# Where weights start, and how many rows the norm factors have, in a two-block fp32 transformer kernel

## The chip, the cores and the metric

The kernel runs on one core of one Trainium2 chip. The metric is the device time of one execution in microseconds. Each timed run gives one such time; the profiled execution is one more run, recorded by the hardware profiler, and it has its own time.

## The reference

Two blocks work on a sequence of 256 tokens of width 1024, in fp32.

```python
def first_block(x, ...):          # one stream
    h = h + hybrid_mixer(rmsnorm(h), w_in, ...)     # dilated attention + state space scan, gated
    h = h + swiglu(rmsnorm(h), w_ffn_in, w_ffn_out) # hidden width 2816
    return rmsnorm(h, final_norm_w)

def second_block(x, c, ctx, c_ctx, ...):            # two streams, x and ctx, and two layers
    for l in range(2):
        mx, mc = split(silu(c) @ w_mod[l] + b_mod[l]), split(silu(c_ctx) @ w_mod[l] + b_mod[l])
        x  = x  + 0.5 * mx[2] * swiglu_2(modulate(rms_norm(x),  mx[0], mx[1]), *ffn1)
        xc = xc + 0.5 * mc[2] * swiglu_2(modulate(rms_norm(xc), mc[0], mc[1]), *ffn1)
        # even layer: windowed attention with sinks, and differential attention:
        #   softmax(q1 k1) - lam * softmax(q2 k2), times v, then rms_norm(y_b, b_sub_norm)
        # odd layer: latent attention (ranks 768 and 256), and neighbourhood attention with a bias table
        # queries and keys of every head are normed: t * rsqrt(mean(t*t) + 1e-6) * gain, then rotated
        ...                                          # out projection, then a second swiglu_2 per stream
```

## The kernel before, in words

**Products.** Activations lie transposed, with features on the 128 partitions and tokens along the row. Every linear layer is computed in three passes of TensorE: a weight and an activation are each split into a rounded part and the rest, and `mm3_k` (L139 to L141) multiplies high by high, high weight by the activation's rest, and the weight's rest by high. In these matmuls the weight block of 128 by 128 is the stationary operand, which is loaded, and the activations are the moving operand, of 256 columns for one stream and 512 for both. In the value units (`v_units`, L1165 to L1167) it is the other way: the weights move, 256 or 320 columns of them, and the activations are loaded.

**Weights.** A weight slab of 128 by 1024 comes by a DMA of the SP queue into one of five buffers (`wraw`, L113). `split_w` casts the high part on ScalarE (L120) and subtracts on VectorE (L121) into one of five pairs of buffers, `wh` and `wl`.

**Units.** A unit is one slab with the outputs that it makes. `run` issues units in order and prepares the slabs of the next two or three. With two streams, the first units (`head`) and the last ones (`edge`) are issued one stream at a time, so that a stream can start while the other isn't ready; all units between take both streams in one matmul of 512 columns.

**Where tiles lie.** A tile's place in SBUF follows from the order in which pools and tiles are declared. `both_acts` declares two tiles that hold both streams side by side (`comb`), from 450 us on; a single stream is half of them. Once the context is no longer needed, `alone` cuts one-stream tiles from the same memory, 48 numbers (192 bytes) further in. The first block's mixer uses tiles of its own. A small `gap` tile after the weights shifts all that is declared behind it.

**Head norms.** `HeadNorm` squares a head's outputs, sums them by matmuls of two columns (L1047), turns the sums to factors, transposes these (L1056), and `finish` spreads each factor over its head's 64, 96 or 128 rows by a matmul (L1071): a selector of zeros and ones (`sel`, 48 rows) is the stationary operand, the factors (`rh`, 48 rows: high parts from row 0, rests from row 32) move, 256 columns. VectorE multiplies. These matmuls are issued among those of the next units.

**Attention.** Steps of heads are woven into one another. `softmax_tail` writes exponentials into one of eight tiles `e`. In the differential attention four heads' outputs are normed by `normed`, which has a square root on ScalarE; ScalarE loads another function table between exponentials and roots (ACT_TABLE_LOAD). In the neighbourhood attention `load_bias` brings a head's table by four DMAs on the SP queue (L1614) and adds a mask on GpSimd (L1615); the scores take it on VectorE (L1623). A scheduler sets the final order on each engine from dependences and buffers.

Of the kernel before, what the change touches and what calls it, by code (L numbers as in the profile page):

```python
# [8 lines left out]
F32 = mybir.dt.float32  # L9
F32R = mybir.dt.float32r  # L10
# [6 lines left out]
T = 256  # L17
# [31 lines left out]
class Unit:  # L49


    def __init__(self, src, at, n, body, streams=None, lin=None, wide=False):
        self.src, self.at, self.n, self.body, self.streams, self.lin = src, at, n, body, streams, lin
        self.wide = wide
# [14 lines left out]
class Builder:  # L69
    def __init__(self, ctx, tc, A):  # L70
        self.tc, self.nc, self.A, self.ctx = tc, tc.nc, A, ctx
        nc = self.nc
        self.cst = self.pool(ctx, "cst", 1)
        self.raw_p = self.pool(ctx, "raw", 5)
        self.w_p = self.pool(ctx, "wsplit", 5)

        self.gap(self.pool(ctx, "gap", 1), 320)
        self.tp = self.pool(ctx, "tmp", 10)
        self.small = self.pool(ctx, "small", 2)
        self.comb, self.one_p, self.single = None, None, False  # L80
        self.ps = ctx.enter_context(tc.tile_pool(name="ps", bufs=4, space=PSUM))
        self.pa = ctx.enter_context(tc.tile_pool(name="pa", bufs=2, space=PSUM))
        self.pt = ctx.enter_context(tc.tile_pool(name="pt", bufs=2, space=PSUM))
        self.dram = ctx.enter_context(tc.tile_pool(name="scratch", bufs=1, space=DRAM))
        self.X, self.ACT, self.acc, self.bg, self.deferred = {}, {}, {}, [], []

        self.ones = self.cst.tile([128, 128], F32, name="ones")
        nc.vector.memset(self.ones, 1.0)
        self.cols = self.cst.tile([128, NCOL], F32, name="cols")
        self.ident = self.cst.tile([128, 128], F32, name="ident")  # L90
# [22 lines left out]
        self.nc.sync.dma_start(t[:, :src.shape[1]], src)  # L113
        return t

    def split_w(self, raw, f):
        nc = self.nc
        h = self.w_p.tile([128, 1024], F32R, name="wh")
        lo = self.w_p.tile([128, 1024], F32R, name="wl")
        nc.scalar.copy(h[:, :f], raw[:, :f])  # L120
        nc.vector.tensor_tensor(lo[:, :f], raw[:, :f], h[:, :f].bitcast(F32), op=ALU.subtract)  # L121
        return h, lo
# [79 lines left out]
    def run(self, items, streams, done=None, ko=0, ahead=2):  # L202
# [5 lines left out]
        ready = {}  # L208

        def prepare(i):  # L210
            if i >= len(units) or i in ready:
                return
            u = units[i]
            f = u.src.shape[2]
            ready[i] = [self.split_w(self.load_raw(u.src[j]), f) for j in range(u.at, u.at + u.n)]

        last = {}
        for i, u in enumerate(units):
# [46 lines left out]
        two = len(streams) > 1  # L265
        n, tail, i = len(units), [], 0
        head = ko or (3 if two else 1)
        edge = 0
        while edge < n and sum(u.n for u in units[n - edge - 1:]) <= 3:
            edge += 1  # L270
        for item in items:
# [3 lines left out]
            j, m = i, 0  # L275
            if not two and i < head:

                j = i + 1 if i + 1 < head else n
                prepare(i)
            while j < n and (j < (head if i < head else i + 1) or m + units[j].n <= ahead + 1):  # L280
                prepare(j)
                m += units[j].n
                j += 1
# [804 lines left out]
def head_selectors(K, pool, width, rows, n):  # L1088

    nc, A = K.nc, K.A  # L1090
    at, n2 = COLS[f"sum{width}"]
    sums = K.cols[:rows, at:at + n2]
    raw = K.raw_p.tile([128, 1024], F32, name="wraw")
    sel = pool.tile([48, n * 128], F32R, name=f"sel{width}")
    nc.scalar.dma_start(raw[:48, :n * 128], A[f"sel{width}"])
    nc.vector.tensor_copy(sel, raw[:48, :n * 128])
    return sums, sel


def stacked(K, pool):  # L1100

    zero = K.t1("zero")
    K.nc.vector.memset(zero, 0.0)
    ring = []
    for i in range(4):
        ring.append(pool.tile([48, T], F32R, name=f"rh{i}"))
        K.nc.scalar.copy(ring[i], zero[:48])
    return ring


# [70 lines left out]
def mix_ab(K, streams):  # L1181
    nc, A = K.nc, K.A
    ctx = ExitStack()
# [10 lines left out]
    at = {"x": 0, "c": 256}  # L1194
# [4 lines left out]
    ring = stacked(K, rp)  # L1199
# [42 lines left out]
    sp = K.pool(sx, "abs", 1)  # L1242
# [131 lines left out]
    def normed(po):  # L1374
        yb = sp.tile([128, 4, 128], F32, name="yb", bufs=2)
        nc.scalar.copy(yb, po.rearrange("p (h e) -> p h e", h=4))
        sq = sp.tile([128, 4, 128], F32, name="ybs", bufs=1)
        ss = sp.tile([128, 4], F32, name="yss", bufs=2)


        nc.vector.tensor_scalar(sq, yb, 2.0 ** 64, -2.0 ** 64, op0=ALU.min, op1=ALU.max)
        nc.vector.scalar_tensor_tensor(sq, sq, 2.0 ** -64, sq, op0=ALU.mult, op1=ALU.mult)
        nc.vector.tensor_reduce(out=ss, in_=sq, axis=AX.X, op=ALU.add)
        fin = sp.tile([128, 4], F32, name="fin", bufs=2)
        nc.vector.tensor_scalar(fin, ss, 2.0 ** 64, 2.0 ** -32, op0=ALU.is_lt, op1=ALU.mult)
        nc.vector.tensor_scalar(ss, ss, 1.0 / 128.0, 1e-6 * 2.0 ** -64, op0=ALU.mult, op1=ALU.add)
        nc.vector.reciprocal(ss, ss)
        nc.scalar.activation(ss, ss, AF.Sqrt)
        nc.vector.tensor_tensor(ss, ss, fin, op=ALU.mult)
        nc.vector.tensor_tensor(yb, yb, ss.unsqueeze(2).to_broadcast([128, 4, 128]), op=ALU.mult)  # L1390
        return yb
# [19 lines left out]
def mix_cd(K, streams):  # L1411
    nc, A = K.nc, K.A
    ctx = ExitStack()
# [24 lines left out]
    at = {"x": 0, "c": 256}  # L1438
# [5 lines left out]
    ring = stacked(K, tp)  # L1444
# [3 lines left out]
    raw = {("q", "x"): v8[:, 0:6], ("k", "x"): d8[:, 0:2], ("k", "c"): d8[:, 2:4]}  # L1448
# [105 lines left out]
    sp = K.pool(sx, "cds", 1)  # L1554
# [50 lines left out]
    biases = {}  # L1605

    def load_bias(hd):
        bias = biases[hd] = sp.tile([128, 2, T], F32, name="bias", bufs=4)
        for t in range(2):
            for rr in range(2):  # L1610
                r = 2 * t + rr
                src = bass.AP(tensor=rpb.tensor, offset=rpb.offset + (hd * 7 + 3 - r) * 127 + 63,
                              ap=[[56 * 127 - 1, 64], [127, 4], [1, 64]])
                nc.sync.dma_start(bias[64 * rr:64 * rr + 64, t].rearrange("p (r c) -> p r c", r=4), src)  # L1614
        nc.gpsimd.tensor_tensor(bias, bias, dmask.unsqueeze(1).to_broadcast([128, 2, T]), op=ALU.add)  # L1615
# [140 lines left out]
def constants():  # L1756
    import numpy as np
    f = np.float32
    c = {}
    i = np.arange(128)  # L1760
# [13 lines left out]
    for g, (c0, n, off, d) in enumerate(((0, 383, 255, 1), (384, 255, 127, 4), (640, 255, 127, 16))):  # L1774
        u = np.arange(n)
        oh[np.where((off - u >= 0) & (off - u <= 128), bucket(np.clip(off - u, 0, 128) * d), 32), c0 + u] = 1.0
    c["onehot"] = oh
    sel = np.zeros((8, 512), f)
# [1 line left out]
        sel[h, h * 64:h * 64 + 64] = 1.0  # L1780
    c["sel"] = sel
    for name, rows, n in (("sel64", [64, 64], 5), ("sel96", [64, 32], 4)):
        sel = np.zeros((48, n, 128), f)
        for b in range(n):
            at = 0
            for e, r in enumerate(rows[:2]):
                sel[[2 * b + e, 32 + 2 * b + e], b, at:at + r] = 1.0
                at += r
        c[name] = sel.reshape(48, n * 128)
    t = np.arange(T)  # L1790

    def rope(dim):
# [129 lines left out]
```

## Time and profile before

| | us |
|---|---|
| timed runs | 2482.21, 2473.56, 2483.57 |
| their median | 2482.21 |
| profiled execution | 2473.19 |
| its span, first to last instruction | 2471.4 |

The page gives busy time by engine and the chain of waits that ended last. The mean granted TensorE clock is 0.985 of full speed. In the timeline each row is one instruction (or a group of equal ones), with start and duration; matmuls are pipelined, so the time of one is read from its start to the next one's start. PE is TensorE's matmuls, PEld its weight loads. In names such as `48*128 48x256` the first pair is the rows and columns of the stationary tile, the second the moving operand.

### The profile page before, as it was taken

How to read it: one execution, taken by the hardware profiler on the slowest of the kernel's cores; microseconds unless marked ns; L12 is line 12 of the kernel's file. 1: busy time of each engine (PE TensorE's matmuls, PEld its weight loads, DVE VectorE, ACT ScalarE, POOL GpSimd, SP SyncE). 2: the span in 40 equal slices, each digit the busy share in tenths (PEclk: the TensorE clock that was granted, in tenths of full speed). 3: DMA queues.
4: the chain of work that ended last, by engine and by line, in shares of the span. 5: the costliest groups of instructions: out<-in, count | busy, mean ns of one | idle time of the engine just before them, and what ended most of it. 6: DMA issues, size and time to landing. Idle time of an engine off the chain costs nothing.

```text
span 2471.4 us, 38395 instructions
## 1 busy us (share of the span) xinstructions
PE 2415.3 (98%) x15104; PEld 2101.6 (85%) x15104; DVE 1642.8 (66%) x3016; ACT 1064.7 (43%) x1934; POOL 34.3 (1%) x56
## 2 busy tenths in 40 slices
PE   7999999999999999999999999999999999999999
PEld 6998999999988888886498888888888888876999
DVE  5767787787865666778757666656555555667655
ACT  4566565535632222535743222243222234555443
POOL 3000000000000000000000000000000000000000
PEclk9999899999999999999899999999999999999999
DMA  9455455676454554341014555534555422233554
GB/s 271 153 154 157 134 175 174 212 251 225 148 177 136 170 173 144 112 139 52 1 52 154 165 159 162 165 108 142 180 166 171 150 87 84 100 97 86 169 195 133
DMA packets 113157, 363.38 MB, mean 147 GB/s; under 512 B 21186, under 2 KB 23562, under 8 KB 112976
## 3 DMA queue, kind: packets, MB, share of 16 engines
q1 hardware_dynamic: 109232, 352.58, 45.1%
q0 software_dynamic: 2176, 5.09, 0.9%
q10 hardware_dynamic: 1568, 3.25, 0.4%
q8 instruction: 119, 1.95, 0.3%
q14 instruction: 62, 0.51, 0.1%
HBM read 359.33 MB, written 3.36 MB: 147 GB/s over the span
## 4 chain that ended last, share of the span: by engine, by line
PE 70%; DVE 3%; ACT 2%; issue 1%; DMA 0%; ACTq 0%; DVEq 0%
PE pm L139 20%; PE pm L140 20%; PE pm L141 20%; PE pt L1140 1%; PE pa L1047 1%; PE pm L1339 1%; PE pt L1071 1%; PE pa L1592 1%; DVE wl L121 1%; PE pm L1600 1%; PE pa L1355 1%; PE pm L1279 1%; PE pa L1316 0%; PE pm L1622 0%; PE pm L1165 0%
## 5 line engine op out<-in xcount | busy, mean ns | idle before, releaser
L139 PE MATMUL pm<-ah,wh 128*128 128x256 f32 (+2 forms) x3096 | 1002.9, 326 | 13.1 <-ACT ah L370 10.7
L140 PE MATMUL pm<-al,wh 128*128 128x256 f32 (+2 forms) x3096 | 997.4, 323 | 1.1 <-DVE al L371 1.0
L141 PE MATMUL pm<-ah,wl 128*128 128x256 f32 (+2 forms) x3096 | 996.1, 322 | 0.0
L120 ACT CAST wh<-wraw 128x1024 fp32r<-128x1024 f32 (+4 forms) x535 | 541.0, 1014 | 946.0 <-PE pm L140 750.3
L121 DVE TENSOR_TENSOR wl<-wraw,wh 128x1024 fp32r<-128x1024 f32 (+4 forms) x535 | 627.5, 1176 | 228.3 <-ACT wh L120 225.8
L139 PEld LDWEIGHTS pm<-ah,wh 128*128 128x128 f32 (+1 forms) x3096 | 590.1, 192 | 67.8 <-ACT ah L370 12.3
L140 PEld LDWEIGHTS pm<-al,wh 128*128 128x128 f32 (+1 forms) x3096 | 591.9, 191 | 49.0 <-issue 2.7
L141 PEld LDWEIGHTS pm<-ah,wl 128*128 128x128 f32 (+1 forms) x3096 | 592.2, 191 | 46.6 <-issue 2.3
L140 PE MATMUL pm<-hl,wh 128*128 128x512 f32 (+1 forms) x934 | 312.6, 335 | 0.0
L139 PE MATMUL pm<-hh,wh 128*128 128x512 f32 (+1 forms) x934 | 312.1, 334 | 0.0
L141 PE MATMUL pm<-hh,wl 128*128 128x512 f32 (+1 forms) x934 | 312.1, 334 | 0.0
L1001 DVE SCALAR_TENSOR_TENSOR junk<-wraw,cactc 128x1024 f32<-128x1024 f32 x112 | 137.2, 1225 | 183.1 <-DMA wraw<-w_mod 183.0
L1001 DVE SCALAR_TENSOR_TENSOR junk<-wraw,cactx 128x1024 f32<-128x1024 f32 x144 | 176.1, 1223 | 48.8 <-DMA wraw<-w_mod 46.2
L139 PEld LDWEIGHTS pm<-hh,wh 128*128 128x128 f32 x934 | 175.7, 188 | 18.7
L140 PEld LDWEIGHTS pm<-hl,wh 128*128 128x128 f32 x934 | 175.7, 188 | 18.6
L141 PEld LDWEIGHTS pm<-hh,wl 128*128 128x128 f32 x934 | 175.8, 188 | 18.4
L125 ACT CAST hh<-g 128x512 fp32r<-128x512 f32 (+1 forms) x113 | 59.1, 525 | 228.4 <-DVE g L428 228.4
L428 DVE TENSOR_TENSOR g<-g,pm 128x512 f32<-128x512 f32 (+1 forms) x113 | 64.0, 567 | 55.6 <-PE pm L141 54.1
L126 DVE TENSOR_TENSOR hl<-g,hh 128x512 fp32r<-128x512 f32 (+1 forms) x113 | 63.9, 567 | 0.3
L458 DVE SCALAR_TENSOR_TENSOR xc<-pm,mcol0c,xc 128x256 f32<-128x256 f32 x56 | 26.9, 481 | 53.5 <-PE pm L141 53.3
L424 ACT ACTIVATE g<-pm 128x512 f32<-128x512 f32 (+1 forms) x116 | 55.9, 486 | 2.0 <-PE pm L141 2.0
L1140 PEld LDWEIGHTS pt<-ident,e 128*128 128x128 f32 x272 | 30.7, 145 | 22.0 <-issue 18.6
(425 smaller groups left out, 2260.0 us busy)
## 6 DMA issues: line engine op xcount, KB each, us to landing
wraw<-w_mod SPq DMA_DIRECT2D x144, 512.0 KB, 4.0
wraw<-f1g SPq DMA_DIRECT2D x44, 512.0 KB, 3.9
wraw<-f1u SPq DMA_DIRECT2D x44, 512.0 KB, 4.2
wraw<-f2g SPq DMA_DIRECT2D x44, 512.0 KB, 3.6
wraw<-f2u SPq DMA_DIRECT2D x44, 512.0 KB, 3.6
wraw<-f1d SPq DMA_DIRECT2D x32, 512.0 KB, 3.9
wraw<-f2d SPq DMA_DIRECT2D x32, 512.0 KB, 3.6
wraw<-w_xbc SPq DMA_DIRECT2D x24, 512.0 KB, 3.7
```

Of the source, the lines that this page charges most:

```text
L120: nc.scalar.copy(h[:, :f], raw[:, :f])
L121: nc.vector.tensor_tensor(lo[:, :f], raw[:, :f], h[:, :f].bitcast(F32), op=ALU.subtract)
L125: self.nc.scalar.copy(h, src)
L126: self.nc.vector.tensor_tensor(lo, src, h.bitcast(F32), op=ALU.subtract)
L139: nc.tensor.matmul(out, h[:, c], ah, start=first, stop=False)
L140: nc.tensor.matmul(out, h[:, c], al, start=False, stop=False)
L141: nc.tensor.matmul(out, lo[:, c], ah, start=False, stop=last)
L424: nc.scalar.activation(half(g["g"], s), p, AF.Silu)
L428: nc.vector.tensor_tensor(t, t, p, op=ALU.mult)
L458: self.nc.vector.scalar_tensor_tensor(x, p, gate, x, op0=ALU.mult, op1=ALU.add)
L1001: nc.vector.scalar_tensor_tensor(junk, raw, 1.0, K.cact[s], op0=ALU.mult, op1=ALU.mult, accum_out=K.mcol[layer, s][:, j:j + 1])
L1140: nc.tensor.transpose(p[:, j * 128:(j + 1) * 128], b, K.ident)
```

## The change

The buffers of split weights grow from 1024 to 1088 numbers per row. A unit that takes one stream from the tiles of both (with two streams: units of one stream, and the head and edge units; with one stream: units whose activations are half of `comb`) gets its weights 16 numbers, 64 bytes, further into the buffer. The gap tile shrinks from 320 to 64 bytes. The selectors and factors of the head norms become tiles of 128 rows, zero beyond the rows used before; the selector's host table grows with them. The square in `normed` takes a tile of the ring `e` in place of its own buffer, and the bias tables have three buffers in place of four.

```diff
-        self.gap(self.pool(ctx, "gap", 1), 320)
+        self.gap(self.pool(ctx, "gap", 1), 64)
...
-    def split_w(self, raw, f):
+    def split_w(self, raw, f, at=0):
         nc = self.nc
-        h = self.w_p.tile([128, 1024], F32R, name="wh")
-        lo = self.w_p.tile([128, 1024], F32R, name="wl")
+        h, lo = (self.w_p.tile([128, 1088], F32R, name="w" + n)[:, at:at + 1024] for n in "hl")
...
-            ready[i] = [self.split_w(self.load_raw(u.src[j]), f) for j in range(u.at, u.at + u.n)]
+
+            if two:
+                alone = len(u.streams or streams) == 1 or i < head or i >= n - edge
+            else:
+                alone = self.comb and not self.single and u.lin and u.lin[0] == self.acts
+            ready[i] = [self.split_w(self.load_raw(u.src[j]), f, 16 if alone else 0) for j in range(u.at, u.at + u.n)]
...
-    sel = pool.tile([48, n * 128], F32R, name=f"sel{width}")
-    nc.scalar.dma_start(raw[:48, :n * 128], A[f"sel{width}"])
-    nc.vector.tensor_copy(sel, raw[:48, :n * 128])
+    sel = pool.tile([128, n * 128], F32R, name=f"sel{width}")
+    nc.scalar.dma_start(raw[:, :n * 128], A[f"sel{width}"])
+    nc.vector.tensor_copy(sel, raw[:, :n * 128])
...
-        ring.append(pool.tile([48, T], F32R, name=f"rh{i}"))
-        K.nc.scalar.copy(ring[i], zero[:48])
+        ring.append(pool.tile([128, T], F32R, name=f"rh{i}"))
+        K.nc.scalar.copy(ring[i], zero)
...
-        sq = sp.tile([128, 4, 128], F32, name="ybs", bufs=1)
+        sq = sp.tile([128, 512], F32, name="e", tag="e", bufs=8).rearrange("p (h e) -> p h e", h=4)
...
-        bias = biases[hd] = sp.tile([128, 2, T], F32, name="bias", bufs=4)
+        bias = biases[hd] = sp.tile([128, 2, T], F32, name="bias", bufs=3)
```

The lines of the new kernel are numbered four higher from the norms on. Each engine's instructions stand in the same order as before, but for the differential attention and the end of the neighbourhood attention.

In the differential attention, ScalarE's order around the third root (before L1388, after L1392; exponentials are L1120 and L1124, the scaling of a probability is L1345 and L1349). Before:

```order
L1120 ACTIVATE e,bd<-pm,bm 128x512
L1388 ACT_TABLE_LOAD
L1388 ACTIVATE yss<-yss 128x4
L1345 ACTIVATE e<-e,bd 128x512 x2
L1145 COPY pts<-pt 128x512
L1368 ACTIVATE ah<-pt,gsub 128x4x128
L318 ACTIVATE acc<-xc 128x256
L1145 COPY pts<-pt 128x512
L1376 COPY yb<-pa 128x512
L321 ACTIVATE sq<-xc 128x256
L1388 ACTIVATE yss<-yss 128x4
```

After, the same place:

```order
L1392 ACT_TABLE_LOAD
L1392 ACTIVATE yss<-yss 128x4
L1124 ACT_TABLE_LOAD
L1124 ACTIVATE e,bd<-pm,bm 128x512
L1149 COPY pts<-pt 128x512
L1124 ACTIVATE e,bd<-pm,bm 128x512
L1349 ACTIVATE e<-e,bd 128x512
L1124 ACTIVATE e,bd<-pm,bm 128x512
L322 ACTIVATE acc<-xc 128x256
L1349 ACTIVATE e<-e,bd 128x512
L1149 COPY pts<-pt 128x512
L1372 ACTIVATE ah<-pt,gsub 128x4x128
```

The third root moved ahead of the last exponentials, so that the table of exponentials is loaded again behind it, and the fourth root, further down, loads its own.

On the SP queue, the loads of the neighbourhood bias (L1614 before, L1618 after) and the second feed-forward's first weights (`f2g`, `f2u`). Before:

```order
L1604 DMA dmask<-dmask 128x256
L1614 DMA bias<-rpb 64x4x64 x16
L113 DMA wraw<-f2g 128x1024
L113 DMA wraw<-f2u 128x1024
L1614 DMA bias<-rpb 64x4x64 x16
```

After:

```order
L1608 DMA dmask<-dmask 128x256
L1618 DMA bias<-rpb 64x4x64 x12
L113 DMA wraw<-f2g 128x1024
L113 DMA wraw<-f2u 128x1024
L1618 DMA bias<-rpb 64x4x64 x20
```

The fourth head's four DMAs moved from ahead of the two weight loads to behind them.

## Rows read from the trace of the kernel before

**Rows 1.** The page: busy time, share and instructions of engines; chain by engine.

```profile
PE 2415.3 (98%) x15104; PEld 2101.6 (85%) x15104; DVE 1642.8 (66%) x3016; ACT 1064.7 (43%) x1934; POOL 34.3 (1%) x56
...
PE 70%; DVE 3%; ACT 2%; issue 1%; DMA 0%; ACTq 0%; DVEq 0%
```

**Rows 2.** Timeline of TensorE, two stretches: start us, duration us, engine, line, operation.

```profile
539.75 0.28 PE L139 MATMUL pm<-ah,wh 128*128 128x256 f32 x1
...
542.99 0.28 PE L139 MATMUL pm<-ah,wh 128*128 128x256 f32 x1
...
2369.82 0.28 PE L140 MATMUL pm<-al,wh 128*128 128x256 f32 x1
...
2373.00 0.28 PE L141 MATMUL pm<-ah,wl 128*128 128x256 f32 x1
```

**Rows 3.** Stretches: length, busy us (x records) by engine, PEclk, DMA share, GB/s.

```profile
30.00:48.00 18.00, 18.00 (x155) 18.00 (x155) 8.90 (x8) 10.30 (x16) 9.77 (x19) 1.00 0.99 235
536.00:578.00 42.00, 41.98 (x349) 41.69 (x348) 37.44 (x60) 20.19 (x31) 0.00 (x0) 1.00 0.77 261
700.00:1000.00 300.00, 300.00 (x1325) 248.43 (x1324) 188.24 (x288) 78.66 (x100) 0.00 (x0) 1.00 0.49 154
1220.00:1230.00 10.00, 10.00 (x30) 6.14 (x28) 4.30 (x13) 3.97 (x10) 0.00 (x0) 0.50 0.00 0
2361.00:2402.00 41.00, 41.00 (x364) 41.00 (x363) 23.84 (x30) 20.14 (x30) 0.00 (x0) 1.00 0.61 193
```

**Rows 4.** Timeline of TensorE, matmuls of 512 columns after an interruption, two stretches.

```profile
1078.15 0.40 PE L140 MATMUL pm<-al,wh 128*128 128x512 f32 x1
...
1078.86 0.40 PE L140 MATMUL pm<-al,wh 128*128 128x512 f32 x1
...
2106.09 0.39 PE L141 MATMUL pm<-hk,wl 128*128 128x512 f32 x1
...
2107.03 0.95 PE L1047 MATMUL pa<-cols,sq 128*128 128x2 f32 x8
```

**Rows 5.** Timeline of TensorE around a head norm's factor matmul (L1071).

```profile
2116.73 0.28 PE L139 MATMUL pm<-hq,wh 128*96 128x256 f32 x1
2116.93 0.38 PE L1071 MATMUL pt<-rh,sel 48*128 48x256 f32 x1
2117.25 0.36 PE L140 MATMUL pm<-lq,wh 128*96 128x256 f32 x1
2117.44 0.28 PE L141 MATMUL pm<-hq,wl 128*96 128x256 f32 x1
```

**Rows 6.** Timeline of the weight loads of the same stretch.

```profile
2116.93 0.18 PEld L1071 LDWEIGHTS pt<-rh,sel 48*128 48x128 f32 x1 [0.16 <-issue]
...
2117.33 0.16 PEld L141 LDWEIGHTS pm<-hq,wl 128*96 128x96 f32 x1
```

**Rows 7.** Timeline of TensorE, two other changes of instruction.

```profile
2119.81 0.28 PE L141 MATMUL pm<-hq,wl 128*96 128x256 f32 x1
2119.93 0.95 PE L1047 MATMUL pa<-cols,sq 128*128 128x2 f32 x8
...
2258.27 0.65 PE L1592 MATMUL pa<-pts,vd 128*64 128x256 f32 x4
2258.85 0.39 PE L141 MATMUL pm<-ah,wl 128*128 128x256 f32 x1
2259.07 0.28 PE L139 MATMUL pm<-ah,wh 128*128 128x256 f32 x1
```

**Rows 8.** Weight loads of L1071: ns min/median/max, first and last start, forms.

```profile
L1071 PEld LDWEIGHTS pt<-rh,sel x64: 129/182/186, 1077.4 to 2187.3; 48*128 48x128 f32 x38, 48*64 48x64 f32 x16, 48*96 48x96 f32 x10
```

**Rows 9.** Timeline of ScalarE in the differential attention.

```profile
1211.45 1.28 ACT L1388 ACT_TABLE_LOAD   x1
```

**Rows 10.** Timelines of GpSimd and VectorE in the neighbourhood attention.

```profile
2229.41 1.27 POOL L1615 TENSOR_TENSOR bias<-bias,dmask 128x512 f32<-128x512 f32 x1 [27.20 <-DMA bias<-rpb]
...
2230.38 0.43 DVE L1623 TENSOR_TENSOR pm<-pm,bias 128x256 f32<-128x256 f32 x1 [0.42 <-PE pm L1622]
```

More of the change, by code (lines that the diff above doesn't have):

```diff
@@ L1782, in constants @@
     for name, rows, n in (("sel64", [64, 64], 5), ("sel96", [64, 32], 4)):
-        sel = np.zeros((48, n, 128), f)
+        sel = np.zeros((128, n, 128), f)
         for b in range(n):
@@ L1788, in constants @@
                 at += r
-        c[name] = sel.reshape(48, n * 128)
+        c[name] = sel.reshape(128, n * 128)
     t = np.arange(T)
```

## Prediction

> **What bounds the kernel now.** I read the page's busy time first, then its chain of waits: TensorE works for 98% of the span, and 70% of the chain that ended last are TensorE's own instructions, the next engine having 3% [rows 1]. So a nanosecond saved on a matmul is a nanosecond off the end, unless it lies in a stretch where TensorE waits for somebody. The question is then what a matmul costs, and the durations don't tell it: matmuls are pipelined, so their 0.28 us overlap, and one has to read from start to start. In the timeline, 27 matmuls of 256 columns go from 539.75 to 542.99, which is 120.0 ns each; 28 of the same line, names and shape go from 2369.82 to 2373.00, which is 113.6 ns each [rows 2]. The stage table says that this isn't chance of three microseconds: 42 us hold 349 matmuls in the one place (120 ns), 41 us hold 364 in the other (113 ns), at the same full granted clock and with TensorE busy throughout; a third stretch, at 30 us, lies between (18 us by 155 less the one that straddles the edge is 117 ns) [rows 3].
>
> What differs is where the operands start in SBUF. From the tile declarations (positions in bytes, modulo 128): the split weights begin at 64 everywhere. A tile that holds both streams begins at 64. The tiles of one stream (the first block's first activations, the last layer's "alone" tiles, cut 192 bytes further in) begin at 0. The 120 ns stretch pairs 64 with 64, the 113 ns stretch pairs 0 with 64. I matched all 15104 matmuls of the trace to the program's addresses: the equal pair is always at 120; the unequal one is at 113.4 for some three quarters and at 117 to 118 for the rest.
>
> **Part 1, weights 64 bytes further.** A longer buffer adds 256 bytes, ten buffers 2560, the smaller gap takes 256 back: 2304 is 18 times 128, so every other tile keeps its position. Only units that run one stream from a tile of both change their pair: 2580 matmuls of 256 columns in mm3_k (1056 of them in the first block's feed-forward, from 456 to 626 us), and in the value units, where the weights are the moving side, 192 of 256 and 192 of 320 columns. They go from equal to unequal by 64. The 4782 matmuls of 512 columns stay with an equal pair (226.6 ns, 300 us by 1324 [rows 3]) and the 5208 that are unequal already stay so. A further 144, of c_uq, go from (96, 64) to (96, 0), both off by an odd 32: nothing, within 5 ns each, 0.7 us.
>
> Price: three parts of 113.6 and one of 117 make 114.5, so 5.5 ns less than 120.0. Times 2772 that is 15.2 us, and if the 320-column ones save the same 5.5 ns, 1.1 us more: together 16 us. The trace has unequal pairs only with the weights at 64 and the activations at 0; now the weights are at 0 and the activations at 64. Whether that mirror is worth the same no row shows. Bounds: at the best 6.4 ns for all 2964, 19 us; at the 117 ns of the 30 us stretch, 3 ns, 9 us; nothing at all; and below nothing, because one unequal pair is not fast: the keys' rank tile (96 against 64) with 512 columns takes 235 ns (four intervals from 2106.09 to 2107.03), 8 above the usual 227. But those runs are short, and an equal pair straight after an interruption shows 237 (three intervals from 1078.15 to 1078.86) [rows 4], so this end is weak: 8 ns by 2964 is 24 us slower. I take the 5.5 ns, since the place that the trace moves from slow to fast is the relative one.
>
> Cover: faster matmuls help only if nothing else becomes late. In the densest stretch VectorE is busy 37.4 of 42 us and the DMA share is 0.77 [rows 3]; 5.5 ns less per matmul makes the stretch 40.1 us, still over 37.4, and the share 0.81, under the 0.99 of the stretch at 30 us, where TensorE is busy throughout as well. If VectorE or DMA did hold that stretch, at most the 2 us that it gives would go.
>
> The Trainium skill, "SBUF — State Buffer", section "Who interferes with whom", gives TensorE two independent read ports, one for the moving operand and one for weights, and says that it never waits on anyone; by that the place of a tile could not matter and this part would be 0, which is the sum of rival A below. The trace does not agree: 120.0 against 113.6 for the same shape.
>
> **Part 2, factors on 128 rows.** The factor matmul (L1071) uses 48 rows. Between 128-row matmuls it costs more than its columns: L139 starts at 2116.73, L1071 at 2116.93, L140 at 2117.25, L141 at 2117.44 [rows 5]. That is 0.71 us for three that take 0.35 elsewhere, 0.36 too much. The weight loader shows why: L1071's load starts at 2116.93, with its matmul and after an idle 0.16, while L141's starts at 2117.33, 0.11 before its own matmul at 2117.44 [rows 6]. A load of another tile size waits for the running matmul; one of the same size overlaps. The neighbours without a change of rows bear this out: L1047, on 128 rows, starts 0.12 after the L141 before it, at 2119.93; and a 128-row tile of 64 columns (L1592) is again followed by 0.22 instead of 0.114 [rows 7]. So a tile of 128 rows and over 64 columns joins the others. Of the 64 factor matmuls 38 have 128 and 10 have 96 columns; the 16 of 64 columns keep a size of their own [rows 8]. Some of the 48 stand in pairs, whose second one pays little; over the trace their excess sums to 15 us, 315 ns each. I take 14, for what stays of a load behind a two-column matmul (L1047's loads are exposed anyway). Bounds: 15 gained; or nothing, if the load waits for another reason; 128 rows to load instead of 48 do not make the load longer, as L141's on 128 rows and 96 columns takes 0.16 and L1071's on 48 rows and 128 columns 0.18 [rows 6]. The setup grows by nothing on the path: more partitions, the same length per partition, done long before the first use.
>
> The Trainium skill, "TensorE: Matmul & The Clock Gate", section "The mechanism", says that a weight load overlaps a running matmul only where the row groups differ; by that 128 rows would gain nothing and this part would be 0, the sum of rival B below. The trace does not agree: L141's load, on all 128 rows, runs beside L140's matmul on the same rows.
>
> **Part 3, buffers that change owner.** The square of the differential attention's sub-norm now takes one of the eight tiles of the probabilities, and the scheduler orders that stage anew. The order of ScalarE has one more pair of table loads, since an exponential now follows the third root. A load is 1.28 us, so 2.6 us at most if both lie on the path, as at 1211.45, where ScalarE loads a table amid the stage [rows 9]. Behind that stall ten microseconds run at half clock (0.50, the 1.2 GHz level [rows 3]), which is 5 us of full clock lost. I take 1; the ends are a gain of 3, if the new order takes a pair off the path, and a loss of 10: 2.6 for the pair, as long again for what waits behind it, and 5 for another spell at half clock.
>
> The bias has three buffers for four. Now the fourth head's tables wait for the first head's release, as the fifth's do before: the fifth's mask add stood 27.20 us for its DMA and began at 2229.41, so the tables were ready at 2230.68; the fourth head's scores take theirs at 2230.38 [rows 10]. That is 0.3 us late, and once more for the eighth, 1 us in all. SP's next weight loads stand ahead of the waiting issue in both orders, so the feed-forward's slabs behind it wait no longer than before.
>
> **Sum.** −16 −14 +1 +1 is −28, on the profiled execution: 2473.2 us, of which the span is 2471.4. That gives 2445. The timed runs of before lie at 2473.6, at the profile's own time, and twice at 2482 to 2484, 9 above it; the median is one of the high ones. The same for the change is 2445 to 2454. I predict 2448.
>
> **Rivals.** *Only the relative place in before's one form counts* (A): the mirror pair stays at 120, part 1 is 0: 2473 − 14 + 2 is 2461. For it: no row shows the weights at 0. Against: the value units, with the roles changed, are at 120 too while equal. *The factor loads stay exposed* (B): the 48 keep their 0.3 us, part 2 is 0: 2473 − 16 + 2 is 2459. For it: after L1047 an L139 shows a gap as well. Against: rows 6 and 7. *The new order of the differential attention costs a stall more* (C): 10 instead of 1, so 2454. For it: the extra loads; against: the square no longer waits for the one buffer of the square before it. *The mirror is worse than the equal pair* (D): the matmuls at one stream pay up to 8 ns more, as the rank tile seems to: +24 − 14 + 2 is +12, 2485. It decides from about 4 ns a matmul, where the 12 us of part 2 and 3 are eaten up. For it: 235 against 227; against: with 256 columns the queries' rank tile, paired the same, takes 0.12 (2119.81 to 2119.93 [rows 7]), no more than an equal pair.
>
> **How the numbers follow.** Forecast 0.60; A 0.12; B 0.11; C 0.11; D 0.06. Half a percent, 12.4 us, is about what a measurement of this kernel can tell from no change. Against the median of 2482, the forecast, and A, B and C where the timed runs are as before, are beyond it; where the high level doesn't come again or several cases meet, they aren't far: of A, B and C I give a third to no change, 0.11, and of D half, with the other half slower. With a little for what I don't see: faster 0.83, same 0.12, slower 0.05. The likeliest case alone spans 2436 to 2456, by the 9 to 19 us of part 1 and the two levels of the runs; the range for 8 in 10 reaches to A, B and C with the high level, 2470, and down to 2430, where the matmuls save 6.4 ns and the reordered stage closes a stall.
>
> **What would show it.** In the changed kernel's timeline, matmuls at 540 us should start every 113 to 118 ns, with 360 to 370 in a 42 us stretch; the 512-column ones stay at 227. The factor matmul should start 0.12 after its predecessor, its load ahead of it. If the starts at 540 us stay at 120.0, A holds; if L1071 still begins with its load, B; if half-clock slices grow around 1215 to 1240, C. The prediction is wrong if the first block's feed-forward, 456 to 626 us, does not get about 6 us shorter.

## The result and the profile after

The changed kernel takes 2444.41 us in the median of four runs (2441.64 to 2453.54), before takes 2478.95 us in the median of four. The ratio is 0.9863, with a 95% interval of 0.9831 to 0.9895. In a second session (six runs beside twelve of before) the ratio was 0.992, 0.9894 to 0.9945. The intervals meet around 0.989, some 26 us less. The forecast was 28 us less. But two of its terms were wrong, in opposite directions, so the total is right by luck and the single stages have to be looked at.

The profiled execution of the changed kernel took 2453.54 us with a span of 2451.7, so it is the slowest of its four; what one profile can and cannot say is taken up below. First the page, as in [rows 1]:

```profile
PE 2385.8 (97%) x15104; PEld 2088.3 (85%) x15104; DVE 1641.5 (67%) x3016; ACT 1066.2 (43%) x1936; POOL 34.2 (1%) x56
...
PE 68%; DVE 3%; ACT 2%; issue 1%; DMA 0%; SPq 0%; POOL 0%; ACTq 0%; DVEq 0%; POOLq 0%
```

TensorE's busy time fell by 29.5 us, from 2415.3, but the span only by 19.7: it now waits more. Where it became faster the timeline of TensorE shows. The first block's feed-forward, as in [rows 2] (start us, duration us):

```profile
533.91 0.28 PE L138 MATMUL pm<-ah,wh 128*128 128x256 f32 x1
...
539.44 0.28 PE L140 MATMUL pm<-ah,wl 128*128 128x256 f32 x1
539.75 0.36 PE L138 MATMUL pm<-ah,wh 128*128 128x256 f32 x1
...
540.41 0.28 PE L140 MATMUL pm<-ah,wl 128*128 128x256 f32 x1
...
547.89 0.28 PE L140 MATMUL pm<-ah,wl 128*128 128x256 f32 x1
```

From 533.91 to 539.44 there are 47 intervals, 117.7 ns each; then 0.31 to the next start; from 540.41 to 547.89 there are 66, 113.3 ns each. The same line, the same tiles' places, the same shape, and two speeds with an interruption between. Before, these matmuls had one speed, 120.0. The prediction's count for this place, 360 to 370 matmuls in 42 us, did not come. There are 337, and TensorE was idle for 2.3 us of the 42:

```profile
534.00:576.00 42.00, 39.68 (x337) 38.88 (x336) 35.87 (x56) 16.42 (x24) 0.00 (x0) 1.00 0.74 257
```

The factor matmuls (L1071, now L1075) as in [rows 5], in the same stretch of the queries:

```profile
2105.07 0.28 PE L138 MATMUL pm<-hq,wh 128*96 128x256 f32 x1
2105.19 0.28 PE L1075 MATMUL pt<-rh,sel 128*128 128x256 f32 x1
2105.30 0.28 PE L139 MATMUL pm<-lq,wh 128*96 128x256 f32 x1
2105.42 0.28 PE L140 MATMUL pm<-hq,wl 128*96 128x256 f32 x1
```

Now 0.12, 0.11 and 0.12 instead of 0.20, 0.32 and 0.19. Their weight loads, as in [rows 6]:

```profile
2105.07 0.19 PEld L1075 LDWEIGHTS pt<-rh,sel 128*128 128x128 f32 x1
2105.19 0.16 PEld L139 LDWEIGHTS pm<-lq,wh 128*96 128x96 f32 x1
```

L1075's load starts at 2105.07, 0.12 ahead of its matmul and beside the L138 that runs. All 64 by form (ns min/median/max of one), before and after:

```profile
L1071 PE MATMUL pt<-rh,sel x64: 276/356/384, 1077.4 to 2187.3; 48*128 48x256 f32 x38, 48*64 48x256 f32 x16, 48*96 48x256 f32 x10
```

```profile
L1075 PE MATMUL pt<-rh,sel x64: 277/284/387, 1080.4 to 2165.0; 128*128 128x256 f32 x38, 128*64 128x256 f32 x16, 128*96 128x256 f32 x10
```

The median falls from 356 to 284 ns. The forms are 38, 16 and 10 as in [rows 8], but with 128 rows.

What the waits of TensorE are between 448 and 640 us (who waited for whom: total us, times, longest), before:

```profile
PE pt L345 <- DVE acc L322: 2.7, 1, 2.7
PE pm L139 <- ACT ah L125: 1.4, 1, 1.4
PE pt L353 <- DVE rs L331: 0.8, 1, 0.8
```

and after:

```profile
PE pm L138 <- ACT ah L124: 3.1, 1, 3.1
PE pt L349 <- DVE acc L326: 2.9, 2, 2.8
PE pm L138 <- DVE g L432: 2.3, 3, 1.3
PE pm L138 <- DVE xx L462: 1.3, 1, 1.3
PE pt L357 <- DVE rs L335: 1.0, 2, 0.8
PE pm L139 <- DVE hl L125: 0.7, 1, 0.7
```

What the faster matmuls save is paid back here: there are new waits for VectorE, on the gate product (`g`, 2.3), the residual (`xx`, 1.3) and the split (`hl`, 0.7). The 1.7 more for the first activation (`ah`) are not among them: in a second profile of the same kernel (e5 below) that wait is 1.0 again, and `g` and `xx` are 2.1 and 1.3.

For the differential attention, ten microseconds each (columns as in [rows 3], the clock third from the end), before, and then after, where the same instructions come 3 us earlier at first and 10 us earlier at the end:

```profile
1205.00:1215.00 10.00, 7.88 (x33) 3.57 (x30) 8.71 (x24) 8.58 (x21) 0.00 (x0) 1.00 0.00 0
1215.00:1225.00 10.00, 8.68 (x24) 5.30 (x24) 5.30 (x11) 7.83 (x19) 0.00 (x0) 0.56 0.00 0
1225.00:1235.00 10.00, 9.54 (x38) 5.43 (x36) 4.87 (x16) 4.82 (x7) 0.00 (x0) 0.75 0.00 0
```

and after:

```profile
1205.00:1215.00 10.00, 8.25 (x36) 4.35 (x36) 8.12 (x21) 9.09 (x22) 0.00 (x0) 1.00 0.00 0
1215.00:1225.00 10.00, 8.81 (x51) 5.70 (x50) 7.58 (x20) 9.91 (x21) 0.00 (x0) 1.00 0.00 0
1225.00:1235.00 10.00, 9.07 (x61) 7.03 (x59) 7.66 (x18) 8.84 (x17) 0.00 (x0) 1.00 0.01 2
```

Before, TensorE was busy for 7.88 of ten microseconds and the clock then was granted at 0.56 and 0.75 (at 1.2 GHz for part of the time), which is 6.9 us of full clock lost in twenty. After, it is at 2.4 GHz throughout, and where before had 62 matmul records in the twenty microseconds from 1215 on, after has 112.

For the stages I took the start of the same matmul in both traces and from it the time that a stage lasts, less what it lasted before. All values are differences to the profiled execution of before, in us; stages are named by before's times.

| stage of before | after | e5 (the same) | e2 rows | e3 order | e6 rows, order | e1 place, order | e7 light, all | e8 light, no place |
|---|---|---|---|---|---|---|---|---|
| first block's mixer, 0–448 | −1.2 | +5.5 | −0.1 | −4.1 | −2.4 | −12.6 | −3.5 | +3.2 |
| its feed-forward, 448–640 | +3.5 | −0.1 | +0.7 | −0.7 | −0.3 | −0.4 | −2.3 | −1.1 |
| head norms, 1040–1150 and 2072–2200 | −18.0 | −18.0 | −17.5 | 0.0 | −17.5 | +3.8 | −18.1 | −17.6 |
| both attentions of layer 0, 1150–1265 | −7.0 | −7.1 | +1.4 | −6.6 | −6.5 | −7.0 | −6.9 | −6.6 |
| last feed-forward, 2301–2471 | 0.0 | 0.0 | 0.0 | 0.0 | 0.0 | +6.5 | 0.0 | 0.0 |
| whole span | −19.7 | −18.7 | −14.2 | −8.7 | −21.0 | −9.2 | −35.1 | −22.4 |

The first and the last-but-one row hold no instruction that any of these kernels changes: they say how much two executions differ by themselves. The +3.8 of e1 in the head norms is such a difference too: it is 4.5 us in one stretch, in which the granted clock was 0.62 for ten microseconds, so at 1.2 GHz for part of them.

```profile
2095.00:2105.00 10.00, 10.00 (x42) 7.92 (x42) 5.16 (x16) 4.80 (x13) 0.00 (x0) 0.62 0.27 82
```

### The profile page after: what moved, and what is told of

The parts are those of the page before. It is cut to its first block, busy times and chain, and to the rows that moved or that the text cites. A ratio compares the mean times of both kernels' runs of the same rounds, so it can differ in the third digit from the quotient of the medians.

```text
span 2451.7 us, 38403 instructions
## 1 busy us (share of the span) xinstructions
PE 2385.8 (97%) x15104; PEld 2088.3 (85%) x15104; DVE 1641.5 (67%) x3016; ACT 1066.2 (43%) x1936; POOL 34.2 (1%) x56
## 4 chain that ended last, share of the span: by engine, by line
PE 68%; DVE 3%; ACT 2%; issue 1%; DMA 0%; SPq 0%; POOL 0%; ACTq 0%; DVEq 0%; POOLq 0%
PE pm L138 20%; PE pm L139 20%; PE pm L140 20%; PE pt L1144 1%; PE pa L1051 1%; DVE wl L120 1%; PE pa L1596 1%; PE pm L1283 1%; PE pm L1604 0%; PE pa L1320 0%; ACT e L1124 0%; PE pt L1075 0%; PE pm L1343 0%; DVE al L375 0%; PE pa L1359 0%
## 5 line engine op out<-in xcount | busy, mean ns | idle before, releaser
L138 PE MATMUL pm<-ah,wh 128*128 128x256 f32 (+2 forms) x3096 | 999.6, 325 | 17.9 <-ACT ah L374 11.5
L138 PEld LDWEIGHTS pm<-ah,wh 128*128 128x128 f32 (+1 forms) x3096 | 588.7, 191 | 72.1 <-ACT ah L374 13.3
L138 PE MATMUL pm<-hh,wh 128*128 128x512 f32 (+1 forms) x934 | 312.4, 334 | 1.3 <-DVE xx L462 1.3
L138 PEld LDWEIGHTS pm<-hh,wh 128*128 128x128 f32 x934 | 175.6, 188 | 20.2 <-issue 1.4
```

What stands on the lines that cost most here:

```text
L138: nc.tensor.matmul(out, h[:, c], ah, start=first, stop=False)
```

## The experiments

Each kernel is before or the changed kernel with the edit shown; "ratio" is to before in the same session, by up to seven or twelve runs.

**e1: the place alone.** The diff is the change without the rows on 128 partitions (the longer buffers need the space that the ring and three bias buffers give):

```diff
-    sel = pool.tile([128, n * 128], F32R, name=f"sel{width}")
+    sel = pool.tile([48, n * 128], F32R, name=f"sel{width}")
...
-        ring.append(pool.tile([128, T], F32R, name=f"rh{i}"))
+        ring.append(pool.tile([48, T], F32R, name=f"rh{i}"))
...
```

> The weights 64 bytes further, without the 128-row factors; the square in the ring of the probabilities and three bias buffers are in it, since the longer weight buffers need their space. Theory 1 (an unequal place saves a fixed 5 to 6 ns a matmul, and it reaches the end): 15 us from the place and some 6 from the new order, ratio to before 0.991. Rival (the matmuls get faster, but their stretches then wait for VectorE, so nothing comes of it): the 6 us of the order alone, ratio 0.9975, with TensorE idle for about as long in the first block's feed-forward as its matmuls got shorter.

Measured: 2468.59 us, ratio 0.9997 (0.9973 to 1.0021). Not the 0.991 of theory 1, and against e3, which has the new order alone, no gain at all. The matmuls did get faster (115.2 ns in the mean of uninterrupted groups of twelve, after 119.8), but TensorE waits 3.4 us for VectorE in the feed-forward, on the same tiles as in the changed kernel (`g` 1.9, `xx` 0.9, `hl` 0.6). This profile also has a row that explains why it could hide something: two stretches of e1, the mixer at 230 us and the last feed-forward,

```profile
230.00:270.00 40.00, 39.29 (x312) 34.64 (x311) 36.28 (x73) 23.54 (x48) 0.00 (x0) 1.00 0.44 141
2350.00:2391.00 41.00, 41.00 (x351) 41.00 (x350) 23.31 (x29) 18.81 (x29) 0.00 (x0) 1.00 0.62 187
```

and before's first:

```profile
230.00:270.00 40.00, 38.87 (x200) 32.54 (x199) 26.51 (x52) 16.78 (x36) 0.00 (x0) 0.70 0.21 68
```

Before ran part of the 40 us at half clock (0.70 in the mean) and got 200 matmuls done, e1 312 at full clock: 12.6 us that no edit made. In the last feed-forward e1 has 351 matmuls in 41 us (117 ns), before 364 (113 ns) [rows 3], 6.5 us over the stage, and nothing there was edited either. So the timed ratio says little against 5 us, and e5 and e6 were made to ask again.

**e2: the rows alone.**

```diff
-    sel = pool.tile([48, n * 128], F32R, name=f"sel{width}")
+    sel = pool.tile([128, n * 128], F32R, name=f"sel{width}")
...
-        ring.append(pool.tile([48, T], F32R, name=f"rh{i}"))
+        ring.append(pool.tile([128, T], F32R, name=f"rh{i}"))
...
```

> Selectors and factors on 128 rows, all else as before. Theory 1 (only the tile's rows expose the load, whatever its columns): all 64 factor matmuls lose 0.3 us, pairs less, together 17 to 19 us, ratio 0.993; the 16 of 64 columns start 0.12 after their predecessor like the others. Rival (rows and columns both make the tile's size, as predicted): the 16 keep 0.31, and 12 to 14 us go, ratio 0.995.

Measured: 2454.71 us, ratio 0.9932 (0.9908 to 0.9956), 17 us, theory 1. The stages of the head norms give 17.5 us, and nearly as much in every kernel that has the 128 rows. The 16 of 64 columns lost their exposed load as well.

**e3: the order alone.**

```diff
-        sq = sp.tile([128, 4, 128], F32, name="ybs", bufs=1)
+        sq = sp.tile([128, 512], F32, name="e", tag="e", bufs=8).rearrange("p (h e) -> p h e", h=4)
...
-        bias = biases[hd] = sp.tile([128, 2, T], F32, name="bias", bufs=4)
+        bias = biases[hd] = sp.tile([128, 2, T], F32, name="bias", bufs=3)
```

> Only the square in the ring of the probabilities and three bias buffers: no matmul changes its operands. If the new order of the differential attention is what made that stage 6 to 7 us shorter in the changed kernel, it is here too: ratio 0.9975. If the stage got shorter because of the factors before it, or by where a spell at half clock fell: ratio 1.000, and the prediction's 1 to 2 us slower would be as good.

Measured: 2465.0 us, ratio 0.9988 (0.996 to 1.0016). The timed runs can't tell 6 us from nothing here. The trace can: the stage of the differential attention is 6.6 us shorter, and it is 5.7 to 7.1 shorter in each profiled kernel that has the ring, and 1.4 longer in e2, which hasn't. The neighbourhood attention (2200 to 2265) kept its length to 0.0 us; with three buffers it was 0.0 to 0.4 us longer, and 2.2 once, in the first profile of the changed kernel.

**e4: the place for matmuls of 512 columns too.**

```diff
-            ready[i] = [self.split_w(self.load_raw(u.src[j]), f, 16 if alone else 0) for j in range(u.at, u.at + u.n)]
+            ready[i] = [self.split_w(self.load_raw(u.src[j]), f, 16 if (two or alone) else 0) for j in range(u.at, u.at + u.n)]
```

> The changed kernel, and the weights of the units that take both streams are 64 bytes further too, so that the 4782 matmuls of 512 columns go from an equal to an unequal pair. Theory 1 (a fixed time per matmul, for the place): 4 to 6.7 ns off 227 each, 20 to 32 us less than the changed kernel, ratio to before 0.974 to 0.979. Rival (the place matters only with 256 columns, where the next load has just fitted behind the matmul): the 512-column ones stay at 227, ratio 0.986.

Measured: 2478.99 us, ratio 1.0032 (1.0012 to 1.0052). Neither: it is some 30 us slower than the changed kernel. The stretch of 512-column matmuls:

```profile
700.00:1000.00 300.00, 300.00 (x1288) 240.42 (x1287) 184.25 (x278) 76.67 (x93) 0.00 (x0) 1.00 0.47 152
```

1287 matmuls in 300 us are 233 ns each, for before's 226.6 [rows 3]; 4782 times 6.5 ns is 31 us. The pair that is better with 256 columns is worse with 512. So the place does not save a fixed time per matmul. The rank tile's 235 ns in [rows 4], 32 bytes apart and of 512 columns, had pointed this way.

**e5 and e6: the changed kernel again, and the same with the weights at the old place.**

```diff
-            ready[i] = [self.split_w(self.load_raw(u.src[j]), f, 16 if alone else 0) for j in range(u.at, u.at + u.n)]
+            ready[i] = [self.split_w(self.load_raw(u.src[j]), f, 0) for j in range(u.at, u.at + u.n)]
```

> The changed kernel once more, as the measure for the next three. All theories: 2443 to 2450, ratio to before 0.987 to 0.990.

> The changed kernel with all weights at the old place: 128-row factors, the new order and the longer buffers stay. Theory 1 (the place saves 4 ns a matmul but what it saves is waited for elsewhere): the same as the changed kernel within 3 us, without the waits for VectorE in the first block's feed-forward. Rival (the place is worth its 11 us and the single profiles hid it): 9 to 12 us slower than the changed kernel.

Measured: e5 2448.07 us, ratio 0.992 (0.9894 to 0.9945); e6 2454.9 us, ratio 0.994 (0.9917 to 0.9963). The medians are 6.8 us apart, the intervals overlap. That lies between theory 1 and the rival. In the traces the feed-forward is no shorter with the place (−0.1 against −0.3). Without the first and the last stage of the table, e5's profile is some 5.5 us shorter than e6's. But 2.9 us of that lie in two stretches (1010 to 1040 and 2265 to 2301 of before) in which the clock was down for longer in e6. First e5, then e6:

```profile
1030.00:1045.00 15.00, 12.41 (x94) 12.13 (x93) 10.29 (x37) 7.17 (x19) 0.00 (x0) 0.89 0.25 84
2258.00:2276.00 18.00, 13.36 (x94) 12.83 (x93) 11.33 (x26) 7.79 (x14) 0.00 (x0) 0.81 0.26 89
```

```profile
1022.00:1037.00 15.00, 12.70 (x82) 12.41 (x82) 10.68 (x38) 7.39 (x20) 0.00 (x0) 0.77 0.25 87
2256.00:2274.00 18.00, 13.37 (x84) 12.84 (x82) 10.47 (x23) 6.84 (x14) 0.00 (x0) 0.72 0.25 80
```

Some 2.5 us are left for the place, in pieces of under a microsecond in other one-stream stretches.

**e7 and e8: the same two with little work on VectorE beside the first block's feed-forward.**

```diff
-                nc.vector.scalar_tensor_tensor(junk, raw, 1.0, K.cact[s], op0=ALU.mult, op1=ALU.mult,
+                nc.vector.scalar_tensor_tensor(junk[:, :256], raw[:, :256], 1.0, K.cact[s][:, :256], op0=ALU.mult, op1=ALU.mult,
...
```

Both kernels have this edit; e8 has that of e6 as well.

> The changed kernel, with the modulation products that VectorE computes beside the first block cut from 1024 to 256 columns (this leaves three quarters of each modulation sum out). Against e8: theory 1 (VectorE holds the first block's feed-forward): with VectorE light, the matmuls from 448 to 640 start every 115.7 ns without waits, and the stretch is 4 to 6 us shorter than in e8. Rival (something else holds it, DMA or the slabs): it is as long as in e8.

> As e7 (modulation products cut to 256 columns), with all weights at the old place. Matmuls of one stream at 120 ns, no waits in the first block's feed-forward; theory 1: 4 to 11 us slower than e7; rival: the same as e7.

Measured: e7 2438.98 us, ratio 0.988 (0.9856 to 0.9904); e8 2450.1 us, 0.9917 (0.9892 to 0.9943). TensorE's waits in e7 between 448 and 640 us:

```profile
PE pt L349 <- DVE acc L326: 2.9, 2, 2.8
PE pm L138 <- ACT ah L124: 1.0, 1, 1.0
PE pt L357 <- DVE rs L335: 1.0, 2, 0.8
PE pm L140 <- DVE wl L120: 0.2, 1, 0.2
```

The waits for `g`, `xx` and `hl` are gone, as theory 1 had it. The stage table of the 192 us of before, after, e7 and e8 (third value with its count: VectorE):

```profile
448.00:640.00 192.00, 186.76 (x1554) 185.70 (x1553) 153.01 (x249) 95.71 (x148) 0.00 (x0) 0.98 0.66 217
```

```profile
448.00:640.00 192.00, 180.68 (x1522) 178.45 (x1521) 149.95 (x244) 91.78 (x142) 0.00 (x0) 0.97 0.64 213
```

```profile
448.00:640.00 192.00, 187.89 (x1583) 186.82 (x1584) 131.86 (x255) 98.28 (x152) 0.00 (x0) 0.97 0.67 225
```

```profile
448.00:640.00 192.00, 187.16 (x1564) 186.30 (x1563) 129.25 (x249) 95.88 (x147) 0.00 (x0) 0.98 0.66 218
```

With VectorE busy some 130 us the place brings TensorE from 1564 matmuls (e8) to 1583 (e7). With VectorE's full work, some 150 us, it brings nothing: 1556 in e6, and in the changed kernel 1552 (e5) or 1522 (its first profile, which also waited 2.1 us longer for `ah`). So VectorE is what held it. The gain is smaller than theory 1 had it, though: e7's feed-forward is 1.2 us shorter than e8's, not 4 to 6. Its timeline, at three places of a stretch without a gap:

```profile
460.43 0.28 PE L139 MATMUL pm<-al,wh 128*128 128x256 f32 x1
...
505.43 0.28 PE L138 MATMUL pm<-hh,wh 128*128 128x256 f32 x1
...
556.43 0.28 PE L139 MATMUL pm<-al,wh 128*128 128x256 f32 x1
```

To 505.43 there are 397 intervals of 113.3 ns, from there 433 of 117.8, and none is over 0.12 us: the speed changed where the hidden activations (`hh`, `hl`) took over. Where nothing interrupts them, the 1056 matmuls of the changed place took 115.8 ns in the mean, for 119.9 in e8, which saves some 4.2 us, as theory 1 had it. But the 338 of `hh` and `hl` in this stretch, whose place the change leaves alone, took 116.0 for 113.5, which costs 0.8, and short pauses cost some 2 more. That loss is not e7's alone: those 338 took 113.5 to 113.8 ns in each profile without the place and 114.1 to 117.8 in each one with it. The 11 us between the two timed medians are for the most part not from there; between the two profiles 6.7 us lie in the mixer, where nothing differs.

**e9 and e10: 64 and 96 rows.**

```diff
-    sel = pool.tile([128, n * 128], F32R, name=f"sel{width}")
+    sel = pool.tile([64, n * 128], F32R, name=f"sel{width}")
...
-        ring.append(pool.tile([128, T], F32R, name=f"rh{i}"))
+        ring.append(pool.tile([64, T], F32R, name=f"rh{i}"))
...
```

> The changed kernel with selectors and factors on 64 rows. Theory (a load is exposed where the tile's row count differs from the running one's; 48 rows are held in a tile of 64): the factor matmuls start 0.2 after their predecessor and take 0.31 again, load and matmul starting together; TensorE from before's 1040 us to 2200 us about 17 us longer than in the changed kernel. Rival (zero-padding beyond 48 rows is what helps, at any size): 0.12 like the changed kernel.

> The changed kernel with selectors and factors on 96 rows. Theory: 96 rows are held in a tile of 128, so it is like the changed kernel, factor matmuls 0.12 after their predecessor. Rival (only exactly the neighbours' 128 rows help): 0.2 and 0.31 as before.

One profiled run each; e9 took 2470.24 us, e10 2454.62. All factor matmuls by form, of e9:

```profile
L1075 PE MATMUL pt<-rh,sel x64: 275/356/576, 1076.4 to 2177.7; 64*128 64x256 f32 x38, 64*64 64x256 f32 x16, 64*96 64x256 f32 x10
```

and of e10:

```profile
L1075 PE MATMUL pt<-rh,sel x64: 278/285/388, 1078.0 to 2162.2; 96*128 96x256 f32 x38, 96*64 96x256 f32 x16, 96*96 96x256 f32 x10
```

64 rows have before's median, 356 ns; 96 rows have the changed kernel's, 285 for 284. The stages of the head norms: e9 +0.8 us, e10 −18.1. Both came out as the theory had it.

**e11: 32 bytes in place of 64.**

```diff
-            ready[i] = [self.split_w(self.load_raw(u.src[j]), f, 16 if alone else 0) for j in range(u.at, u.at + u.n)]
+            ready[i] = [self.split_w(self.load_raw(u.src[j]), f, 8 if alone else 0) for j in range(u.at, u.at + u.n)]
```

> The changed kernel with the weights of one-stream units 32 bytes further instead of 64: their pair is 64 against 32, as the rank tiles' 96 against 64. Theory (any pair that isn't equal leaves the 120 ns): matmuls of 256 columns at 113 to 118 as in the changed kernel, time equal within 3 us. Rival (64 bytes apart is what counts): 118 to 120 throughout and 3 to 7 us slower than the changed kernel.

Measured: 2447.65 us, ratio 0.9914 (0.9883 to 0.9944). The timeline of the feed-forward, first and last of 413 matmuls without a gap:

```profile
456.94 0.28 PE L138 MATMUL pm<-ah,wh 128*128 128x256 f32 x1
...
505.70 0.28 PE L140 MATMUL pm<-ah,wl 128*128 128x256 f32 x1
```

412 intervals are 118.3 ns each: this pair shows one speed, near the slower one of the two. So the size of the offset counts, as the rival had it; the time doesn't show it, as theory had it, since so little of the saving reaches the end.

**e12: the split on GpSimd**, as a try at a better version.

```diff
-                self.split(*part(j, s), t)
+                h, lo = part(j, s)
+                self.nc.scalar.copy(h, t)
+                eng = self.nc.gpsimd if len(streams) == 1 and not self.single else self.nc.vector
+                eng.tensor_tensor(lo, t, h.bitcast(F32), op=ALU.subtract)
```

> The changed kernel, with the rest of the hidden activations (t minus its rounded part, 22 of 256 columns) of the first block's feed-forward computed on GpSimd and not on VectorE. Theory 1 (VectorE is late there): some 6.6 us less for VectorE, the waits for it between 448 and 640 shrink from 5 to 2 us, and the kernel is 2 to 4 us faster than the changed one. Rival (GpSimd and VectorE get in each other's way, or the queue's order and not its load makes the waits): no gain or some us slower.

Measured: 2448.14 us, ratio 0.9902 (0.9877 to 0.9928), no faster than the changed kernel. The first of TensorE's waits between 448 and 640 us:

```profile
PE pm L138 <- DVE g L432: 2.3, 4, 1.1
PE pm L138 <- ACT hh L436: 1.0, 1, 1.0
PE pm L138 <- DVE xx L465: 0.9, 1, 0.9
PE pm L139 <- POOL hl L438: 0.9, 1, 0.9
```

The waits for `g` stay and one for GpSimd comes. Taking 22 small subtractions off VectorE is too little or in the wrong place; the rival's second half is not excluded. None of the twelve is a version clearly faster than the changed kernel with all its work done.

## Why the prediction came out right, point by point

- **The bound.** Right: TensorE's time was the currency. Where its matmuls started closer together and no wait followed, the stage became shorter.
- **Rows on 128 partitions: −14, measured −17.5** (stages) and −17 (e2). The mechanism was right, the load that waits for a tile of another size. Its step "a tile of 128 rows and over 64 columns joins the others", by which the 16 of 64 columns were to keep their stall, failed: it is the rows alone (e2, e9, e10). In the changed kernel a 64-column one costs 0.35 us with its two neighbours for 0.66 before, 0.31 each and 5 us for the 16. By the means of such threes the other 48 lost 13.6 us, so the 14 for them was right and the 16 are what it lacked. L1592, from which I argued in [rows 7], differs from the others by something else than its 64 columns; what, I didn't try. Rival B (loads still exposed) is refuted.
- **Weights 64 bytes further: −16, measured between 0 and −7**, by the timed medians of e1 against e3 (+4) and of e5 against e6 (−7); −11 with VectorE light. This term was mis-sized in three ways. The price was 4.1 ns and not 5.5: over the trace the new pair is at 118 ns about as often as at 113, 115.7 in the mean, 119.8 before, and its neighbours of an unchanged pair got slower with it. The 320-column ones gained nothing (146.6 after 146.5). And the step on the cover, "still over 37.4 … at most the 2 us", failed: a VectorE whose work fills 37.4 of 40.1 us as a sum is late for single products. The 1056 matmuls in the feed-forward save some 5 us (114.9 ns there, after 119.9), and all of it went into waits, pauses and the slower neighbours. The test that I had set, the stretch of 456 to 626 us getting 6 us shorter, went against the prediction: it was 1.2 us longer in the first profile and 0.2 shorter in e5. The traces of e5 and e6 put the place's share near 2.5 us. Rival A (no gain from the place) was nearly right in the place's share and wrong in its reason: the mirror pair does leave the 120 ns.
- **What the prediction cited.** The Trainium skill, "SBUF — State Buffer", section "Who interferes with whom", says that TensorE never waits on anyone. The section is on engines that share ports and names no place of a tile; that the place could therefore not matter was my reading of it. This case shows three speeds for one shape by the place of its tiles (120, 118.3, 113 to 118), and one for 512 columns that goes the other way. The Trainium skill, "TensorE: Matmul & The Clock Gate", section "The mechanism", says that a load overlaps a running matmul only where the row groups differ. The trace does not agree: the load on 128 rows at 2105.07 runs beside a matmul on the same rows. The same section also lets a load go ahead into a background weight buffer, which I had left out, so that rival B did not follow from it. What the runs show is that loads on 96 and 128 rows overlap here, and those on 48 and 64 among them don't.
- **The order: +1, measured −6.6** in the stage. I had counted the extra pair of table loads (2.6 us) and not what else the new order does: TensorE's stall is shorter (8.25 busy of ten microseconds for 7.88 at its worst here), and no half-clock spell follows. The spell of before cost 6.9 us by the clock of its two rows, as much as the whole gain: I had counted what another spell would cost, and not that the one in [rows 3] could go. That the one is the cause of the other is my reading; that both are gone with the ring, and only with it, e2 and e3 show. I had its price among the bounds of the range as a gain of 3 and had taken the other side. Rival C is refuted.
- **Three bias buffers: +1, measured 0.0** in e3, 0.0 to 0.4 in most others.
- **Rival D**, the mirror pair worse by 8 ns, is refuted for 256 columns. With 512, where the change doesn't use the pair, it is 6.5 ns worse.
- **The chances.** By the shares given to A, B, C and D, no change comes to 0.14, and not to the 0.12 that is stated.

So the sum was right by luck, because two errors cancel: the place gave some 12 us less than I took, rows, order and bias together some 12 more.

Open: why the place sets the pace at all, and what sets whether a run of 256-column matmuls goes at 113 or at 118; the timed runs leave the place's own share at 0 to 7 us.

## What to carry to other kernels

Between matmuls whose stationary tiles fill 128 rows, give every small one 128 rows as well, with zeros: its load then hides, here 0.3 us each, with 64, 96 or 128 columns alike. Try a tile's start in SBUF at each width by itself, for what is faster at 256 columns was slower at 512. And before counting a faster matmul as time, ask which busy engine in that stretch delivers its operands, here VectorE with 37.4 us of work for 40.1: a sum that fits is not a schedule that fits.

## What the runs showed of the hardware

- A matmul's pace depends on the places of both operands in SBUF, modulo 128 bytes: 256 columns take 120.0 ns with equal places, 118.3 with 32 bytes apart, 113 or 118 with 64 bytes apart; 512 columns take 226.6 with equal places and 233 with 64 bytes apart.
- The pair 64 bytes apart has two speeds. It changed between them at an interruption (117.7 before the pause at 539.44, 113.3 after it), and also with no gap at all, where another tile of activations took over (113.3 to 117.8 at 505.43 in e7).
- The load of a factor matmul on 96 or 128 rows overlaps the running matmul on 128 rows; on 48 or 64 rows it starts only with its own matmul, and the matmul's median rises from 284 to 356 ns.
- Executions differ by the spells at 1.2 GHz that they fall into. From 230 to 270 us, where before and e1 run the same instructions, before had 200 matmuls in 40 us (clock 0.70) and e1 312 (clock 1.00). That is 12 us, more than any part of this change but one. Two profiles of the changed kernel differ by 6.7 us in the stage that holds this stretch.
